# Attention with adaLN: the 24 conditioning products of the attention stage, tied to softmax steps one by one

## The chip, the cores and the metric

One core of one Trainium2 chip runs the kernel. The metric is device time in microseconds (us) of one execution; the times shown are medians of several executions. Matmuls run on TensorE (PE; PEld is its weight load), elementwise work on VectorE (DVE), ScalarE (ACT) and GpSimd (POOL). DMA transfers are issued from the queues of SyncE (SP) and GpSimd.

## The reference, cut to what matters

A decoder trunk of two layers, 512 tokens of width 1024: attention and a feed-forward block, then a gated DeltaNet and a feed-forward block. Every sub-layer is preceded by an RMSNorm whose scale and shift, and followed by a gate, that come from the condition vector c (adaLN):

```python
cond = jax.nn.silu(c)
for layer in range(DEPTH):
    mod = (cond @ ada_w[layer] + ada_b[layer])[:, None, :]
    shift_m, scale_m, gate_m, shift_f, scale_f, gate_f = jnp.split(mod, 6, axis=-1)
    h = rmsnorm(x, norm_mix_g[layer]) * (1.0 + scale_m) + shift_m
    mixed = attention_head_groups(h, ...) if layer % 2 == 0 else gated_deltanet(h, ...)
    x = x + gate_m * mixed
    h = rmsnorm(x, norm_ffn_g[layer]) * (1.0 + scale_f) + shift_f
    x = x + gate_f * swiglu(h, ffn_w_in[layer], ffn_w_out[layer])
```

The attention has eight softmax heads (MoBA) and eight stick-breaking heads of width 64 over the same 512 tokens, causal.

## The kernel before, in words

Everything is f32; a matmul is made of three, on operands split into a high and a low part (`split`, line 246, writes the high part on ACT and the low part on DVE).

The matrix-vector product of adaLN is not done on TensorE. `ada` (line 206) loads a block of 128x1024 weights (tile `aw`, 512 KB, issued from SP), and one DVE instruction multiplies it by `cond` and adds up along the row (line 214), with a second short one that writes the sum to a column of `mod`. There are 96 such blocks: 6 components times 8 chunks for each layer. The first 16 (shift and scale of the first norm) run at the start, 24 run in the attention stage (components 2, 3 and 4 of the first layer: the gate of the attention, shift and scale of the first feed-forward block), and 56 run in the first feed-forward block. In the attention stage `aw` has two buffers, so the load for one product can be issued only when the product two before it has run, and SP, which takes its queue in order, waits there.

The attention stage goes over four pairs p of heads, and over two heads h in each (called head 1 to head 8 here). A head is a softmax head, `moba` (line 749), followed by a stick-breaking head, `stick` (line 774). `moba` has four steps, one per block of 128 queries. A step is a chain across the engines: scores on PE (tile `s`, one buffer), the row maximum on DVE (line 759), the exponential with its row sum on ACT (line 761), the reciprocal on DVE (line 762), the scaling of the row by it on DVE (line 763, tile `p`), transposes on PE (line 767, tile `pt`, one buffer) and their split into `ph` and `pl`. Four steps done, `pv_out` multiplies by the values. `stick` is such a chain too, with tiles `z`, `u`, `ssh`, `ssl`, `sph`, `spl`.

While the chains of a pair run, PE has other matmuls in between: the projections of the next pair (`proj`, line 707; `spread` in line 702 ties each group of three matmuls to a matmul of a step), and in heads 7 and 8 a part of the output projection (lines 840 to 842). The weights of the projections come on GpSimd's queue, each in two transfers (lines 286 and 288, `wh` and `wl`); those of the output projection (`attn_out`, tile `raw`, line 292) come on SP's queue behind the `aw` loads.

Which instruction follows which on an engine is settled when the program is built, by a scheduler that simulates the engines and takes ready instructions by their place in the source. `tc.issue_after(x)` makes what stands in its block come after instruction x on x's engine. On the chip each engine runs its list strictly in order, and waits for semaphores.

Before the change `moba` returns the reciprocal of its last step, and the loop over heads places products after it, as many as the table says (lines 72 and 814 to 817):

```python
ADA = (0, 6, 6, 6, 6, 0, 0, 0)
```

so that six products are placed after the last softmax step of each of heads 2 to 5. `between` (line 830) would place what the table leaves over; the table leaves none.

Of the kernel before, what the change touches and what calls it, by code (L numbers as in the profile page):

```python
# [12 lines left out]
AF = mybir.ActivationFunctionType  # L13
OP = mybir.AluOpType
# [53 lines left out]
OG, NG = (6, 8), 18  # L68
GS = 4
ROT = 2  # L70
AENG = "v"
ADA = (0, 6, 6, 6, 6, 0, 0, 0)
NSPLIT = 4
NFIRST = 2
NFIRST_GDN = 2
# [55 lines left out]
def build(nc, tc, I, O):  # L131
    V, G, A, PE = nc.vector, nc.gpsimd, nc.scalar, nc.tensor
    from contextlib import ExitStack
    ctx = ExitStack()
    with ctx:
# [38 lines left out]
        apool = actx.enter_context(tc.tile_pool(name="apool", bufs=1))  # L174
        cond = apool.tile([128, D], F32, name="cond")
# [27 lines left out]

        mod = const.tile([128, 96], F32, name="mod")

        def ada(layer, comp, chunk, pool=apool, bufs=2, eng="v"):
            j = layer * 48 + comp * 8 + chunk
            w = pool.tile([128, D], F32, name="aw", tag="aw", bufs=bufs)
            nc.sync.dma_start(w, I["ada_w"][j])
            if eng == "g":  # L210
                ins = G.tensor_tensor(w, w, cond, op=OP.mult)
                A.activation(w, w, AF.Copy, accum_out=mod[:, j:j + 1])
                return ins
            return V.tensor_tensor_reduce(w, w, cond, 1.0, 0.0, OP.mult, OP.add, mod[:, j:j + 1])  # L214

        fin = const.tile([128, 96], F32, name="fin")
# [240 lines left out]
        env.__dict__.update(locals())  # L457

        xctx = attention(env, xctx)
        with ExitStack() as fctx:  # L460
            after = norm(1, 0, 1, hs)
# [73 lines left out]
def attention(e, x0ctx):  # L535
    nc, tc, V, G, A, PE, I = e.nc, e.tc, e.V, e.G, e.A, e.PE, e.I
    from contextlib import ExitStack
    with ExitStack() as ctx:
# [73 lines left out]
        with e.psum_pool("start") as sp:  # L612
            pq = [sp.tile([128, T], F32, name=f"pq{i}") if i < 1 else e.mm_tile() for i in range(4)]
            pv = [sp.tile([128, T], F32, name=f"pv{i}") for i in range(4)]
            with e.pool("rtmp") as tmp:
                for k in range(KC):
# [7 lines left out]
                    ins = e.norm_h(FULL, 0, 0, 1, hs, (k,))  # L624
# [3 lines left out]
                    a, z = k == 0, k == KC - 1  # L628
# [73 lines left out]
        def spread(n, u0, u1):  # L702

            s = [x for u in range(u0, u1) for x in steps[u]]
            e.gates[:] = [s[i * len(s) // n] for i in range(n)]

        def proj(pair, i):
            w = e.load_w(("attn_in", (pair - 1) * 4 + i))
            ps = e.mm_tile()
            e.gemm(ps, w, hs, FULL)  # L710
            return finish(ps, *KINDS[i])

        def vproj(i):
            ws = [e.load_w(("attn_v", i, j)) for j in (0, 4)]
            for c in range(4):
                ps = e.mm_tile()[:, :256]
                t = slice(c * 128, c * 128 + 128)
                for k in range(KC):
                    xh, xl = hs[k]
                    wh, wl = (w[:, k % 4] for w in ws[k // 4])  # L720
                    with e.behind() if k % 2 == 0 else ExitStack():
                        PE.matmul(ps, xh[:, t], wh, start=k == 0, stop=False)
                        PE.matmul(ps, xh[:, t], wl, start=False, stop=False)
                        PE.matmul(ps, xl[:, t], wh, start=False, stop=k == KC - 1)
                for j in range(2):
                    e.split(ps[:, j * 128:j * 128 + 128], *(t[:, c] for t in vtile("b", 2 * i + j)))

        def pv_out(chunk, r0, tag, ph, pl, at):

            o = psum.tile([128, T], F32, name="o", tag="o", bufs=1)  # L730
            vh, vl = vtile("ab"[chunk // 4], chunk % 4)
            for j in range(4):
                q = slice(j * 128, T)
                PE.matmul(o[:, q], vh[:, j], at(ph, j), start=j == 0, stop=False)
                PE.matmul(o[:, q], vl[:, j], at(ph, j), start=False, stop=False)
                PE.matmul(o[:, q], vh[:, j], at(pl, j), start=False, stop=j == 3)
            rs = slice(r0, r0 + 64)
            e.split(o[rs], ot[chunk][0][rs], ot[chunk][1][rs])

        def qk3(ps, k, ks, q, qs, at, mask):  # L740

            kh, kl = k
            qh, ql = q
            PE.matmul(ps, kh[:, ks], qh[:, qs], start=True, stop=False)
            PE.matmul(ps, kh[:, ks], ql[:, qs], start=False, stop=False)
            PE.matmul(ps[:, at], e.identb, mask, start=False, stop=False)
            steps[-1].append(PE.matmul(ps, kl[:, ks], qh[:, qs], start=False, stop=True).ins)

        def moba(pair, h, q, k):

            ph = work.tile([128, 1920], F32R, name="ph", tag="ph", bufs=1)
            pl = work.tile([128, 1920], F32R, name="pl", tag="pl", bufs=1)
            for i in range(4):
                n = 128 * (i + 1)
                qs = slice(i * 128, n)
                s = psum.tile([128, T], F32, name="s", tag="s", bufs=1)
                qk3(s[:, :n], q[h], qs, k, slice(0, n), qs, causal)
                st = work.tile([128, 3], F32, name="st", tag="st", bufs=4)
                V.tensor_reduce(st[:, 0:1], s[:, :n], AX.X, OP.max, negate=True)
                p = work.tile([128, T], F32, name="p", tag="p", bufs=2)  # L760
                A.activation(p[:, :n], s[:, :n], AF.Exp, bias=st[:, 0:1], accum_out=st[:, 1:2])
                ins = V.reciprocal(st[:, 2:3], st[:, 1:2])
                V.tensor_scalar(p[:, :n], p[:, :n], st[:, 2:3], None, op0=OP.mult)
                pt = psum.tile([128, T], F32, name="pt", tag="pt", bufs=1)
                for j in range(i + 1):
                    js = slice(j * 128, j * 128 + 128)
                    PE.transpose(pt[:, js], p[:, js], e.ident)
                src = pt[:, :n].rearrange("p (j q) -> p j q", q=128)
                e.split(src, *(x[:, i * 128:i * 128 + 384 * (i + 1)].rearrange("p (j q) -> p j q", q=384)[:, :, :128]
                               for x in (ph, pl)))  # L770
            pv_out(pair, h * 64, "m", ph, pl, lambda x, j: x[:, 512 * j:512 * j + 512 - 128 * j])
            return ins

        def stick(pair, h, q, k):
            off = {3: 0, 2: 128, 1: 384, 0: 768}
# [34 lines left out]
        for p in range(4):  # L810
            qa, ka, qb, kb = cur
            for h in range(2):
                steps.append([])
                ins = moba(p, h, qa, ka)
                for j in range(sum(ADA[:2 * p + h]), sum(ADA[:2 * p + h + 1])):
                    with tc.issue_after(ins.ins):
                        e.ada(0, 2 + j // 8, j % 8, eng=AENG[j % len(AENG)])
                stick(p, h, qb, kb)
            if p == 0:
                vproj(1)  # L820
            if p < 3:
                spread(32, 2 * p, 2 * p + 2)
                cur = [proj(p + 1, i) for i in range(4)]
# [4 lines left out]
        e.open_keep()  # L828

        def between(n, ins):  # L830
            a = sum(ADA)
            m = (24 - a) // 4
            for j in range(a + n * m, a + n * m + m):
                with tc.issue_after(ins.ins):
                    e.ada(0, 2 + j // 8, j % 8)
            if n == 3:
                e.ada_fin(0, 3)
                e.ada_fin(0, 4, gain=e.gffn[:, 0:8])

        s = [x for u in steps[OG[0]:OG[1]] for x in u]  # L840
        for i in range(3):
            e.gates += [s[(6 * i + j) * len(s) // NG] for j in range(6)] + 2 * [None]
        e.out_proj(lambda n: [e.load_w(("attn_out", n, 0))], ot, 0, 2, NSPLIT, e.norm(0, 3, 4, hs),
                   ORDER, between, keep=True)
    return xctx

# [471 lines left out]
```

## Time and profile before

| | |
|---|---|
| median of 3 runs | 1441.11 us (1438.31 to 1442.24) |
| profiled execution: its own time | 1445.06 us |
| profiled execution: span | 1443.2 us (1.86 us of its time lie outside the span) |
| PE busy | 1390.6 us (96%) |
| DVE busy | 831.2 us (58%) |
| ACT busy | 580.3 us (40%) |
| POOL busy | 337.4 us (23%) |

The busy shares are means over the whole span; the attention stage reaches from about 87 to 297 us. Where PE is not busy there, or runs at its lower clock, time is lost that nothing later can win back, as PE has work for nearly all of the rest.

### The profile page before, as it was taken

To read this page: it belongs to the slowest core of one execution; us is meant where nothing else is said; L and a number is where in the kernel's file an instruction comes from. 1 tells how busy PE (TensorE), PEld (TensorE's weight loads), DVE (VectorE), ACT (ScalarE), POOL (GpSimd) and SP (SyncE) were. 2 spreads that over 40 slices of the span, in tenths; PEclk is the share of its full clock that TensorE was granted. 3 is DMA by queue.
4 is the path that set the end of the run, shared out by engine and by line. 5 is a ranking of instruction groups with operands and counts; after the bars stand their busy time and mean duration, and the time that the engine had idled before them with its cause. 6 is when DMAs were issued, how large, how long until landed. Compare 5 with 4: busy or idle time off the path is not lost.

```text
span 1443.2 us, 19371 instructions
## 1 busy us (share of the span) xinstructions
PE 1390.6 (96%) x7418; PEld 1172.9 (81%) x7418; DVE 831.2 (58%) x1410; ACT 580.3 (40%) x1114; POOL 337.4 (23%) x336
## 2 busy tenths in 40 slices
PE   7999898999999999999899989999999999999997
PEld 4787677889888888888878877888998888888887
DVE  6776778646566566423777897436783333333233
ACT  4465565745222222222446743336662222222222
POOL 5023342213111111010424734311031111110010
PEclk8999999999999999999999999999999999999999
DMA  9437664042476666444522314312361332333332
GB/s 369 150 77 181 181 178 129 30 146 89 147 234 225 231 227 216 150 127 124 182 73 74 88 61 130 102 60 88 115 207 45 102 101 90 102 94 92 92 103 74
DMA packets 58734, 190.66 MB, mean 132 GB/s; under 512 B 7081, under 2 KB 11305, under 8 KB 58642
## 3 DMA queue, kind: packets, MB, share of 16 engines
q1 hardware_dynamic: 53376, 173.56, 37.1%
q0 software_dynamic: 4112, 14.82, 4.6%
q8 instruction: 58, 0.95, 0.3%
q10 hardware_dynamic: 1154, 1.05, 0.2%
q14 instruction: 34, 0.28, 0.1%
HBM read 184.11 MB, written 5.29 MB: 131 GB/s over the span
## 4 chain that ended last, share of the span: by engine, by line
PE 80%; DVE 8%; DMA 6%; ACT 3%; POOL 2%; issue 1%; SPq 0%; DVEq 0%; ACTq 0%; POOLq 0%
PE mm L332 20%; PE mm L333 20%; PE mm L335 20%; DMA aw<-in_ada_w_dram 3%; DVE aw L214 1%; PE mm L1126 1%; PE mm L1124 1%; PE mm L1125 1%; PE f L335 1%; PE bank L958 1%; DVE DT L1018 1%; DVE wl L254 1%; PE f L333 1%; PE f L332 1%; DMA call<-in_consts_dram 1%
## 5 line engine op out<-in xcount | busy, mean ns | idle before, releaser
L249 ACT ACTIVATE wh<-raw 128x1024 fp32r<-128x1024 f32 (+1 forms) x199 | 206.9, 1040 | 536.2 <-PE mm L333 493.1
L254 DVE TENSOR_TENSOR wl<-raw,wh 128x1024 fp32r<-128x1024 f32 (+1 forms) x193 | 234.1, 1214 | 195.7 <-ACT wh L249 175.4
L332 PE MATMUL mm<-hh,wh 128*128 128x512 f32 (+1 forms) x776 | 292.4, 381 | 0.2
L333 PE MATMUL mm<-hl,wh 128*128 128x512 f32 (+1 forms) x776 | 291.5, 379 | 0.0
L335 PE MATMUL mm<-hh,wl 128*128 128x512 f32 (+1 forms) x776 | 246.3, 378 | 0.4 <-DVE wl L254 0.4
L333 PEld LDWEIGHTS mm<-hl,wh 128*128 128x128 f32 x776 | 147.0, 190 | 27.6
L332 PEld LDWEIGHTS mm<-hh,wh 128*128 128x128 f32 x776 | 146.9, 190 | 26.9 <-ACT wh L249 0.3
L335 PEld LDWEIGHTS mm<-hh,wl 128*128 128x128 f32 x776 | 142.6, 189 | 29.4 <-DVE wl L254 0.6
L214 DVE CUSTOM_DVE_ANT_0 aw<-aw,cond 128x1024 f32<-128x1024 f32 x96 | 124.1, 1314 | 18.6 <-DMA aw<-in_ada_w_dram 18.5
L251 POOL TENSOR_SCALAR ah<-ac 128x512 fp32r<-128x512 f32 x36 | 53.3, 1481 | 330.4 <-DVE ac L496 330.4
L333 PE MATMUL mm<-al,wh 128*128 128x512 f32 (+1 forms) x354 | 124.6, 356 | 0.0
L332 PE MATMUL mm<-h1h,wh 128*128 128x512 f32 x320 | 124.5, 389 | 0.0
L333 PE MATMUL mm<-h1l,wh 128*128 128x512 f32 x320 | 124.5, 389 | 0.0
L332 PE MATMUL mm<-ah,wh 128*128 128x512 f32 (+1 forms) x354 | 124.2, 356 | 0.1
L496 DVE TENSOR_TENSOR ac<-sg,mm 128x512 f32<-128x512 f32 x40 | 27.5, 687 | 151.5 <-PE mm L335 151.5
L335 PE MATMUL mm<-h1h,wl 128*128 128x512 f32 x320 | 105.0, 389 | 0.0
L335 PE MATMUL mm<-ah,wl 128*128 128x512 f32 (+1 forms) x354 | 104.2, 356 | 0.0
L332 PEld LDWEIGHTS mm<-ah,wh 128*128 128x128 f32 x354 | 66.7, 189 | 9.7 <-ACT ah L249 0.4
L333 PEld LDWEIGHTS mm<-al,wh 128*128 128x128 f32 x354 | 66.8, 189 | 9.6
L335 PEld LDWEIGHTS mm<-ah,wl 128*128 128x128 f32 x354 | 64.2, 189 | 9.6 <-DVE wl L254 0.2
L335 PEld LDWEIGHTS mm<-h1h,wl 128*128 128x128 f32 x320 | 60.1, 188 | 12.5
L333 PEld LDWEIGHTS mm<-h1l,wh 128*128 128x128 f32 x320 | 60.1, 188 | 12.4
(403 smaller groups left out, 2557.7 us busy)
## 6 DMA issues: line engine op xcount, KB each, us to landing
aw<-in_ada_w_dram SPq DMA_DIRECT2D x96, 512.0 KB
raw<-in_ffn_in_dram SPq DMA_DIRECT2D x88, 512.0 KB
raw<-in_ffn_out_dram SPq DMA_DIRECT2D x36, 512.0 KB
raw<-in_gdn_in_dram SPq DMA_DIRECT2D x26, 512.0 KB
raw<-in_gdn_z_dram SPq DMA_DIRECT2D x16, 512.0 KB
raw<-in_gdn_out_dram SPq DMA_DIRECT2D x16, 512.0 KB
raw<-in_ffn_out_dram SPq DMA_DIRECT2D x18, 384.0 KB
wh<-in_attn_in_dram POOLq DMA_DIRECT2D x12, 512.0 KB, 4.1
```

The lines of the kernel that those rows point to most:

```text
L214: return V.tensor_tensor_reduce(w, w, cond, 1.0, 0.0, OP.mult, OP.add, mod[:, j:j + 1])
L249: ins = A.activation(h, src, AF.Copy)
L251: G.tensor_scalar(h, src, 1.0, 1.0, op0=OP.mult, op1=OP.mult)
L254: (G if eng == "p" else V).tensor_tensor(l, src, h.bitcast(F32), op=OP.subtract)
L332: PE.matmul(ps, wh[k][:, 0], xh[:, cs], start=first and i == 0, stop=False)
L333: PE.matmul(ps, wh[k][:, 0], xl[:, cs], start=False, stop=False)
L335: PE.matmul(ps, wl[j][:, 0], x[j][0][:, cs], start=False, stop=last and j == order[-1])
L496: ins = V.tensor_tensor(ac, sg, pu, op=OP.mult)
L958: PE.matmul(ps[:, c], lhs[:, cs], rhs[:, cs], start=True, stop=True)
L1018: V.tensor_tensor(d, DS[:, :m, m:m + 1].to_broadcast([128, m, w]), DV[:, m:m + 1, m:].to_broadcast([128, m, w]), op=OP.mult)
L1124: PE.matmul(p, xh[:, t], wh[:, k - j], start=k == 0, stop=False)
L1125: PE.matmul(p, xl[:, t], wh[:, k - j], start=False, stop=False)
```

## The change

The table and the loop that placed six products after a head's last reciprocal are taken out. Instead each of the four softmax steps of heads 2 to 7 places one product, after its own reciprocal and, in the source, ahead of the scaling. The products, their number (24) and their order are the same. The unused way of doing a product on GpSimd and the empty loop in `between` are removed too.

```diff
-ADA = (0, 6, 6, 6, 6, 0, 0, 0)
+ADA0 = 4
...
                 ins = V.reciprocal(st[:, 2:3], st[:, 1:2])
+                step = 4 * (2 * pair + h) + i - ADA0
+                if 0 <= step < 24:
+                    with tc.issue_after(ins.ins):
+                        e.ada(0, 2 + step // 8, step % 8)
                 V.tensor_scalar(p[:, :n], p[:, :n], st[:, 2:3], None, op0=OP.mult)
...
-                ins = moba(p, h, qa, ka)
-                for j in range(sum(ADA[:2 * p + h]), sum(ADA[:2 * p + h + 1])):
-                    with tc.issue_after(ins.ins):
-                        e.ada(0, 2 + j // 8, j % 8, eng=AENG[j % len(AENG)])
+                moba(p, h, qa, ka)
                 stick(p, h, qb, kb)
...
         def between(n, ins):
-            a = sum(ADA)
-            m = (24 - a) // 4
-            for j in range(a + n * m, a + n * m + m):
-                with tc.issue_after(ins.ins):
-                    e.ada(0, 2 + j // 8, j % 8)
```

Line numbers of the changed program are a little lower: its product is line 209 (before 214), its split's DVE half 249 (254), its reciprocal 757 (762), its scaling 762 (763), the `u` of `stick` 791 (793).

DVE's list before, from the first to the second softmax step of head 4 (`ISA` on `aw` is a product, the `ISA` on `mod` behind it writes its sum; `rq` is a projected q or k under rotation):

```order
L763 TENSOR_SCALAR p<-p,st 128x128
L214 ISA aw,mod<-aw,cond 128x1024
L214 ISA mod 128x1
L668 TENSOR_TENSOR rq<-rq,C 128x512
L254 TENSOR_TENSOR ssl<-u,ssh 128x512
L762 RECIPROCAL st<-st 128x1
L793 SCALAR_TENSOR_TENSOR u<-z,u 128x128
```

The same place of DVE's list in the changed program:

```order
L249 TENSOR_TENSOR ssl<-u,ssh 128x512
L663 TENSOR_TENSOR rq<-rq,C 128x512
L757 RECIPROCAL st<-st 128x1
L209 ISA aw,mod<-aw,cond 128x1024
L209 ISA mod 128x1
L664 TENSOR_TENSOR rq<-rq,rs 128x512
L762 TENSOR_SCALAR p<-p,st 128x256
```

The fifth product of the six placed after head 3 stood ahead of `ssl`, which head 3's stick-breaking part needs, and of the reciprocal; now the second product of head 4 stands between the reciprocal and the scaling, and `ssl` ahead of both. So it is in all 24 steps of heads 2 to 7: one product lies between reciprocal and scaling. Before, 12 of the 24 products lay between a reciprocal and its scaling, in heads 2 to 6, and none in head 7.

DVE's list at the first two steps of head 7, changed program:

```order
L757 RECIPROCAL st<-st 128x1
L209 ISA aw,mod<-aw,cond 128x1024
L209 ISA mod 128x1
L791 SCALAR_TENSOR_TENSOR u<-z,u 128x256
L762 TENSOR_SCALAR p<-p,st 128x128
L249 TENSOR_TENSOR ssl<-u,ssh 128x256
L791 SCALAR_TENSOR_TENSOR u<-z,u 128x384
L249 TENSOR_TENSOR bl_191<-o,bh_190 64x512
L754 TENSOR_REDUCE st<-s 128x1
```

Before, the scaling followed the reciprocal at once here, and no product stood in the head.

SP's queue before, from the loads of the value weights to those of x (a row with x18 is 18 loads in a row):

```order
L292 DMA raw<-in_attn_v_dram 128x1024 x4
L209 DMA aw<-in_ada_w_dram 128x1024 x18
L292 DMA raw<-in_attn_out_dram 128x1024
L209 DMA aw<-in_ada_w_dram 128x1024 x6
L292 DMA raw<-in_attn_out_dram 128x1024 x4
```

The same in the changed program:

```order
L287 DMA raw<-in_attn_v_dram 128x1024 x4
L208 DMA aw<-in_ada_w_dram 128x1024 x16
L287 DMA raw<-in_attn_out_dram 128x1024
L208 DMA aw<-in_ada_w_dram 128x1024
L287 DMA raw<-in_attn_out_dram 128x1024
L208 DMA aw<-in_ada_w_dram 128x1024 x2
L287 DMA raw<-in_attn_out_dram 128x1024
L208 DMA aw<-in_ada_w_dram 128x1024 x3
L287 DMA raw<-in_attn_out_dram 128x1024 x2
L208 DMA aw<-in_ada_w_dram 128x1024 x2
```

The five loads of output-projection weights now stand between the last eight `aw` loads instead of mostly behind them. The last two `aw` loads in either list are for the feed-forward block.

## Rows read from the trace of the kernel before

**Rows 1.** The page: span, and busy time of each engine.
```profile
span 1443.2 us, 19371 instructions
PE 1390.6 (96%) x7418; PEld 1172.9 (81%) x7418; DVE 831.2 (58%) x1410; ACT 580.3 (40%) x1114; POOL 337.4 (23%) x336
```
**Rows 2.** Busy time by stretch: heads 2 to 8, one line each.
```profile
core 0: us, PE busy (x) PEld busy (x) DVE busy (x) ACT busy (x) POOL busy (x), PEclk, DMA share, GB/s
103.70:138.10 34.40, 34.31 (x180) 28.34 (x179) 23.63 (x48) 21.55 (x48) 14.56 (x19) 1.00 0.67 158
138.10:163.90 25.80, 22.98 (x127) 18.41 (x127) 17.37 (x38) 14.44 (x35) 9.02 (x13) 1.00 0.69 197
163.90:192.30 28.40, 24.50 (x125) 20.10 (x124) 22.23 (x45) 15.38 (x37) 11.09 (x12) 0.88 0.62 169
192.30:220.00 27.70, 25.40 (x132) 20.50 (x131) 21.90 (x45) 15.89 (x37) 12.58 (x12) 0.94 0.78 203
220.00:244.40 24.40, 20.49 (x101) 15.93 (x100) 22.89 (x45) 14.47 (x34) 6.97 (x7) 0.95 0.48 160
244.40:264.10 19.70, 19.70 (x116) 16.47 (x114) 11.61 (x27) 13.50 (x34) 3.44 (x6) 0.97 0.17 54
264.10:297.20 33.10, 30.53 (x181) 25.32 (x181) 19.86 (x43) 24.37 (x63) 7.30 (x10) 1.00 0.00 1
```
**Rows 3.** Busy time by stretch: from the end of the attention to the end.
```profile
345.00:1443.00 1098.00, 1074.37 (x5675) 911.69 (x5673) 588.33 (x945) 379.57 (x672) 230.41 (x191) 0.99 0.39 124
```
**Rows 4.** Tile aw, 90 to 345 us: the products and their duration (min/median/max).
```profile
L214 DVE CUSTOM_DVE_ANT_0 aw<-aw,cond x24: 1195/1216/1764, 125.4 to 229.6; 128x1024 f32<-128x1024 f32 x24
```
**Rows 5.** Waits of DVE, 90 to 345 us: us in total, times, longest us.
```profile
DVE aw L214 <- DMA aw<-in_ada_w_dram: 13.2, 7, 4.1
```
**Rows 6.** Timeline at 174 us: start us, us, engine, instruction, [idle before <-releaser].
```profile
175.28 1.22 DVE L214 CUSTOM_DVE_ANT_0 aw<-aw,cond 128x1024 f32<-128x1024 f32 x1 [2.90 <-DMA aw<-in_ada_w_dram]
177.03 0.68 DVE L254 TENSOR_TENSOR ssl<-u,ssh 128x512 fp32r<-128x512 f32 x1
177.77 0.79 PE L799 MATMUL z<-ssl,ntri 128*128 128x512 f32 x1 [3.18 <-DVE ssl L254]
```
**Rows 7.** Timeline, three more waits of PE behind a late DVE, and what held DVE.
```profile
144.35 0.38 PE L744 MATMUL s<-kah,qah 128*128 128x256 f32 x1 [2.01 <-ACT p L761]
...
205.45 1.23 DVE L214 CUSTOM_DVE_ANT_0 aw<-aw,cond 128x1024 f32<-128x1024 f32 x1 [1.45 <-DMA aw<-in_ada_w_dram]
...
207.81 0.73 PE L799 MATMUL z<-ssl,ntri 128*128 128x512 f32 x1 [1.99 <-DVE ssl L254]
...
241.72 0.33 PE L744 MATMUL s<-kah,qah 128*128 128x128 f32 x1 [2.32 <-ACT p L761]
```
**Rows 8.** Busy time by stretch of 4 us: granted clock around waits of PE.
```profile
140.00:144.00 4.00, 2.33 (x16) 1.89 (x14) 1.64 (x4) 0.16 (x1) 0.26 (x1) 1.00 1.03 293
176.00:180.00 4.00, 1.51 (x3) 1.00 (x4) 4.00 (x10) 1.99 (x6) 0.00 (x0) 0.65 0.46 146
180.00:184.00 4.00, 4.00 (x11) 2.80 (x11) 3.94 (x10) 1.26 (x2) 2.21 (x3) 0.50 0.43 135
208.00:212.00 4.00, 4.00 (x12) 2.87 (x13) 3.38 (x8) 1.59 (x6) 1.89 (x2) 0.58 0.91 222
240.00:244.00 4.00, 2.28 (x7) 1.91 (x8) 4.00 (x8) 2.26 (x6) 1.68 (x2) 0.76 0.40 123
244.00:248.00 4.00, 4.00 (x21) 3.35 (x20) 1.51 (x4) 2.12 (x8) 0.22 (x1) 0.82 0.02 8
```
**Rows 9.** Chain that ended last: two transfers of aw, start us, us.
```profile
135.14 10.49 DMA aw<-in_ada_w_dram
...
225.56 4.06 DMA aw<-in_ada_w_dram
```
**Rows 10.** Timeline of DVE in head 7: reciprocals of its first and third step.
```profile
248.09 0.15 DVE L762 RECIPROCAL st<-st 128x1 f32<-128x1 f32 x1
...
257.90 0.15 DVE L762 RECIPROCAL st<-st 128x1 f32<-128x1 f32 x1
```

More of the change, by code (lines that the diff above doesn't have):

```diff
@@ L70 @@
 ROT = 2
-AENG = "v"
-ADA = (0, 6, 6, 6, 6, 0, 0, 0)
+ADA0 = 4
 NSPLIT = 4
@@ L204, in build, with ada @@
         mod = const.tile([128, 96], F32, name="mod")
-        def ada(layer, comp, chunk, pool=apool, bufs=2, eng="v"):
+        def ada(layer, comp, chunk, pool=apool, bufs=2):
             j = layer * 48 + comp * 8 + chunk
@@ L209, in ada @@
             nc.sync.dma_start(w, I["ada_w"][j])
[L210 to L213, printed above, removed]
             return V.tensor_tensor_reduce(w, w, cond, 1.0, 0.0, OP.mult, OP.add, mod[:, j:j + 1])
@@ L771, in moba @@
             pv_out(pair, h * 64, "m", ph, pl, lambda x, j: x[:, 512 * j:512 * j + 512 - 128 * j])
-            return ins
         def stick(pair, h, q, k):
```

## The prediction, made before the changed kernel ran

> **What bounds the kernel now.** I read the page first. PE is busy for 96% of the span, DVE for 58% [rows 1]. The reader should see that no other engine can set the end for the kernel as a whole, so a change of DVE's order can be worth only what PE loses somewhere. After the attention, PE is idle for 1098.00 - 1074.37 = 23.6 us of 1098 at a granted clock of 0.99 [rows 3], and the change touches nothing there. So that part only moves earlier or later as a whole.
>
> The stretches by head come next [rows 2]. In heads 2 and 7 PE is never idle (0.09 us and 0). In heads 3 to 6 it is idle for 25.80 - 22.98 = 2.82, 28.40 - 24.50 = 3.90, 27.70 - 25.40 = 2.30 and 24.40 - 20.49 = 3.91 us, together 12.9 us, and the granted clock drops to 0.88 in head 4. The products placed after heads 2 to 5 run there.
>
> Third, what ends those waits. DVE waits 13.2 us in 7 cases for the load of a product [rows 5]. At 174 us it stands before a product for 2.90 us, runs it for 1.22 us, then does another instruction and the `ssl` of head 3, and only then can PE's next matmul run: PE had waited 3.18 us [rows 6]. At 205.45 it is the same, with 1.99 us of PE waiting [rows 7]. The waits of 2.01 and 2.32 us behind an exponential [rows 7] come from a late row maximum on DVE: at 144 us because of a product that waited for its load, at 241 us because DVE is behind with its list after the last six products (22.89 of 24.40 us busy in head 6 [rows 2]).
>
> Fourth, the clock. After the waits at 174 to 179 us the stretch 180 to 184 us runs at a granted clock of 0.50, that is all at 1.2 GHz, the lower of the two levels; 208 to 212 us has 0.58, 240 to 248 us 0.76 and 0.82 [rows 8]. The work lost in a stretch is half of the time that PE works at the lower level: 4 x 0.50 = 2.0, 4 x 0.42 = 1.7, 4 x 0.24 = 1.0, 4 x 0.18 = 0.7, and for 176 to 180 us, where PE was busy for 1.51 us only, at most 0.75. Together 6.1 us. The 2.01 us wait at 142 us left the clock at 1.00 [rows 8], so a short wait need not cost this.
>
> **The change part by part.** (a) Six products in a burst on two buffers are taken apart. The third to sixth of a burst had to wait for a load that could be issued only when the product two before had run; two such transfers took 10.49 and 4.06 us [rows 9]. With one product per step, the same load has two steps. In head 7, which no product disturbs, reciprocals one and three are 257.90 - 248.09 = 9.8 us apart [rows 10]; less the product, 8.5 us are left for a transfer. That covers the 4.06 us end and falls short of the 10.49 us end by 2.0 us. I take it that most loads arrive in time, and that the waits of PE in heads 3 to 6 go, with the clock they cost: -12.9 - 6.1 = -19.0 us. This is the upper bound of this term as well; its lower bound is 0, should every wait return at another place.
>
> On the load's time the Trainium skill (DMA: Bandwidth & Descriptors, section Bandwidth) states 6.15 us for 1 MB at 341 GB/s, which is two of these loads at once. By that figure, as an estimate, no product would wait at all, and the sum would be 2 us lower than mine, -15.0 us. The trace's 10.49 us for one load speaks for some waits that remain.
>
> (b) What is given back in heads 3 to 6. A product costs DVE 1.22 us [rows 4] and 0.08 us for its sum, so 1.30 us. Now all 24 lie between a reciprocal and its scaling, where 12 did: 12 x 1.30 = 15.6 us longer chains in all, which is the upper bound if PE has nothing else to do in any of them. The lower bound is nothing, from head 2: four products ran in its stretch, one of its scalings stood behind two of them, and PE was idle for 0.09 us [rows 2]. I take 1 us per head, nearer to head 2, because projections lie between the steps there, and half of it for loads that still come late: +4 us. DVE's total work does not change.
>
> (c) Head 7 gets four products that it did not have: 4 x 1.30 = 5.2 us on DVE, 11.61 + 5.2 = 16.8 of 19.70 us, or 85%. Heads 4 and 5 with 78 and 79% lost 3.9 and 2.3 us, partly to the loads. Bounds 0 (PE was never idle here) and 5.2 (nothing hides them); I take 2 us. Head 2's four products stand earlier than before, beside projections that hide them: 0.
>
> (d) The queues. On SP, five loads of output-projection weights now stand between the last eight `aw` loads, so they wait until products of heads 5 to 7 have run. Their first use is at the end of head 6 and in head 7, and the loads of x, which come behind, were issued only at the end of head 8. GpSimd's list hardly changes. 0 us. The removed code on GpSimd was never run: 0. The columns for the feed-forward norm are complete at the end of head 7 instead of in head 6, with all of head 8 (33.10 us [rows 2]) before anything reads them: 0.
>
> Sum: -19.0 + 4 + 2 = -13.0 us. The profiled execution took 1445.06 us, 4.0 us above the median of the runs; against its own time the result is 1432.1, against the median of 1441.11 us it is **1428 us**.
>
> **The rivals.** *The waits stay* (about 1438 us). The `aw` loads compete with GpSimd's transfers of projection weights; in heads 3 to 5 the DMA engines are busy for 62 to 78% [rows 2]. If most transfers then take as long as the 10.49 us one, each product waits about 2 us in its place between reciprocal and scaling, instead of in a burst. DVE waited 13.2 us in all before; 2 us at, say, 6 of the 24 products would nearly restore that, and of the 19.0 us only the backlog of head 6 and its clock would go: 3.9 + 1.7, less 2 in head 7, so about -3.5 us. For it: the load that took 10.49 us. Against it: before, two loads were usually in flight together because products ran back to back, now mostly one. The Trainium skill (DMA: Bandwidth & Descriptors, section Issuing engines are not separate DMA queues) says that transfers of all engines share the same 16 DMA engines and interleave, which is the rule behind this rival; no run here yet shows one load alone.
>
> *The softmax chain becomes the bound* (about 1450 us, slower). Each step of heads 2 to 7 is 1.30 us longer before its transposes can run. If PE runs out of other matmuls in each, the 15.6 us of (b) show in full, and a wait in each of six heads pulls the clock down as at 180 us, 2.0 us each: 15.6 + 12 - 19.0 = +8.6 us. It decides from the point where the waits of a head are long enough to lower the clock, so above the 2 us that left it at 1.00. For it: head 7 has the fewest other matmuls and gets four new products. Against it: heads 2 and 7 show no idle PE at all, and the row maximum and exponential of the next step do not need the scaling of this one.
>
> That the change does not do what it says is excluded: in the order of the changed program each of the 24 reciprocals of heads 2 to 7 is followed by one product.
>
> **How the numbers follow.** About 0.3%, 4.3 us, is what a measurement of this kernel can tell from no change. The forecast, with gains between 6 and 22 us (all of the 19.0, and the 2.6 us that PE idles in head 8 at most), has a chance of 0.72, all of it faster. *The waits stay* has 0.16, half of it just faster and half the same. *The chain* has 0.12, with 0.09 slower and 0.03 the same, where only part of it shows. So faster 0.80, same 0.11, slower 0.09. The range goes from 1419 (22 us gained) to 1439 us, which takes in the first rival and leaves out the second.
>
> **What would show it.** Right: DVE's wait for `aw` well under 13.2 us; PE idle for about 1 us in each of heads 3 to 6 and 2 us in head 7; no stretch at a granted clock near 0.50 in the attention; head 4 shorter than 28.40 us by 4 us or more; the time after the attention unchanged. Wrong: waits of PE for transposes behind a scaling that stands behind a product (the chain), or DVE waiting for loads in many steps (the first rival), or as many microseconds lost again in heads 7 and 8.

## The result, and the profile after

The changed kernel takes 1430.39 us (median of 4 runs, 1428.88 to 1430.72), the kernel before 1439.9 us (median of 4, 1438.31 to 1442.24): a ratio of 0.992 with an interval of 0.9902 to 0.9938. Run again, it took 1429.95 us against 1441.98, 0.9923 (0.9898 to 0.9948). The change makes the kernel 0.8% faster. The prediction was 1428 us in a range of 1419 to 1439. (Further down, one execution of the bursts without loads took 4601.09 us and one with pairs 4674.71; why is open, and leaving them out moves the medians by less than 0.2 us.)

The page of the changed kernel's profiled execution (1430.58 us):

```profile
span 1428.8 us, 19361 instructions
PE 1386.5 (97%) x7418; PEld 1171.3 (82%) x7418; DVE 830.1 (58%) x1410; ACT 581.2 (41%) x1114; POOL 336.8 (24%) x336
```

DVE does the same work as before [rows 1], in a shorter span. Busy time by stretch, heads 2 to 8, columns as in [rows 2]:

```profile
103.10:137.50 34.40, 34.40 (x181) 28.57 (x180) 23.26 (x48) 22.00 (x48) 16.06 (x19) 1.00 0.70 173
137.50:162.10 24.60, 22.79 (x127) 18.74 (x127) 16.94 (x39) 13.68 (x34) 8.18 (x12) 1.00 0.68 187
162.10:185.50 23.40, 22.61 (x129) 18.67 (x128) 20.69 (x42) 16.40 (x40) 9.22 (x12) 1.00 0.69 181
185.50:206.50 21.00, 21.00 (x122) 17.59 (x121) 17.16 (x38) 15.26 (x37) 8.93 (x12) 1.00 0.64 160
206.50:228.90 22.40, 21.35 (x119) 17.54 (x118) 22.04 (x42) 15.25 (x36) 9.03 (x9) 1.00 0.52 160
228.90:249.80 20.90, 20.90 (x127) 17.96 (x126) 18.75 (x42) 15.77 (x40) 8.03 (x9) 1.00 0.53 175
249.80:281.90 32.10, 29.19 (x159) 23.09 (x157) 18.48 (x42) 21.59 (x55) 5.69 (x8) 0.95 0.05 17
```

Heads 3 to 6 took 106.3 us before [rows 2] and take 91.4 us now. PE is idle there for 1.81 + 0.79 + 0 + 1.05 = 3.65 us instead of 12.9, and the granted clock is 1.00 in all four. Head 7, which got four products, is 1.2 us longer, with PE never idle. The time before head 3 is 0.6 us shorter, head 8 is 1.0 us shorter, and what comes behind it takes 1146.9 us instead of 1146.0. The longest waits of DVE (90 to 345 us; us in total, times, longest) and the rows of the products:

```profile
DVE x L405 <- PE mm L330: 10.0, 7, 2.8
DVE u L791 <- ACT u L790: 8.3, 8, 2.2
```
```profile
L209 DVE CUSTOM_DVE_ANT_0 aw<-aw,cond x24: 1195/1206/2323, 105.6 to 247.7; 128x1024 f32<-128x1024 f32 x24
```

The two rows are the longest waits; a row like [rows 5] is not in the list at all: DVE waits for none of the 24 loads. What is new is at the end of head 8, where the stick-breaking chain ends and PE has little else (busy time in stretches of 4 us):

```profile
276.00:280.00 4.00, 2.57 (x7) 1.48 (x7) 0.98 (x2) 1.23 (x2) 0.00 (x0) 0.84 0.00 0
280.00:284.00 4.00, 3.32 (x13) 2.80 (x12) 1.10 (x2) 1.65 (x2) 0.00 (x0) 0.50 0.18 67
284.00:288.00 4.00, 4.00 (x16) 3.22 (x15) 2.99 (x4) 2.64 (x3) 0.00 (x0) 0.81 1.03 338
```

The granted clock drops here, which it did not in the same place before (head 8 at 1.00 [rows 2]). By the prediction's way of counting that is about 4 x 0.16 + 4 x 0.50 + 4 x 0.19 = 3.4 us, less what PE was idle anyway. PE's longest wait there is only 1.35 us. So one of the prediction's signs of being right, no stretch near 0.50 in the attention, did not come.

### The profile page after: what moved, and what is told of

Same layout as the page of the kernel before. It is cut to its first block, busy times and chain, and to the rows that moved or that the text cites. A ratio compares the mean times of both kernels' runs of the same rounds, so it can differ in the third digit from the quotient of the medians.

```text
span 1428.8 us, 19361 instructions
## 1 busy us (share of the span) xinstructions
PE 1386.5 (97%) x7418; PEld 1171.3 (82%) x7418; DVE 830.1 (58%) x1410; ACT 581.2 (41%) x1114; POOL 336.8 (24%) x336
## 3 DMA queue, kind: packets, MB, share of 16 engines
q10 hardware_dynamic: 1154, 1.05, 0.2%
## 4 chain that ended last, share of the span: by engine, by line
PE 83%; DVE 8%; ACT 3%; DMA 3%; POOL 1%; issue 1%; SPq 0%; DVEq 0%; ACTq 0%; POOLq 0%
PE mm L327 21%; PE mm L328 21%; PE mm L330 20%; PE z L797 1%; PE mm L1116 1%; PE mm L1114 1%; PE mm L1115 1%; PE bank L948 1%; PE f L330 1%; DVE DT L1008 1%; DVE wl L249 1%; PE f L328 1%; PE f L327 1%; DMA wh<-in_attn_in_dram 1%; DMA call<-in_consts_dram 1%
## 5 line engine op out<-in xcount | busy, mean ns | idle before, releaser
L348 POOL TENSOR_TENSOR ssq<-ssq,sq 128x512 f32<-128x512 f32 x14 | 21.1, 1508 | 212.1 <-ACT sq L344 212.1
```

The source lines that it names most:

```text
L348: eng.tensor_tensor(ssq[:, cs], ssq[:, cs], sq[:, cs], op=OP.add)
```

## The experiments

Two theories stood after the result. *Loads*: the kernel before lost its time because DVE waited 13.2 us for the loads of products that came in bursts on two buffers. *Burst*: it lost it because a row of products on DVE delays what stands behind the row, wherever the loads are.

A yardstick for all of them is how far PE gets in one fixed stretch, 137.5 to 250 us: the number of its instructions there, the first (x...) in a row. It is read from the profiled execution, which is not always near the median (with pairs it took 1438.49 us, 4 us more than the median), and it does not count what is won or lost outside the stretch. The kernel before:

```profile
137.50:250.00 112.50, 99.57 (x518) 80.38 (x517) 87.05 (x177) 63.81 (x152) 40.41 (x45) 0.94 0.62 175
```

The changed kernel:

```profile
137.50:250.00 112.50, 108.84 (x617) 90.62 (x617) 95.77 (x199) 76.56 (x184) 43.39 (x50) 1.00 0.62 173
```

**Bursts without loads.** The burst of the kernel before, with 22 of the 24 loads left out.

```diff
+        held = {}
...
+            w = held.get(j % 2) if hold else None
+            if w is not None:
+                return V.tensor_tensor_reduce(w, cond, cond, 1e-3, 0.0, OP.mult, OP.add, mod[:, j:j + 1])
...
-                        e.ada(0, 2 + j // 8, j % 8, eng=AENG[j % len(AENG)])
+                        e.ada(0, 2 + j // 8, j % 8, hold=True)
```

> The kernel before, with its bursts of six products, but 22 of the 24 loads in the attention stage are left out: those products multiply cond by itself (scaled by 0.001), so these columns are not the reference's. Same DVE instructions at the same places, nothing to wait for. If the loss of the kernel before came from DVE waiting for loads (loads theory): PE idle in heads 3 to 6 falls from 12.9 us to under 5, time 1429 to 1434 us. If it came from six products standing in a row on DVE, whatever the loads (burst theory): the time stays within 1436 to 1440 us.

Measured: 1448.33 us against 1441.72, ratio 1.0048 (1.0032 to 1.0064). It is slower than the kernel before, which neither theory had. The expectation was wrong in one point: the places were not the same. With no load to wait for, the scheduler packed the six products more closely. The timeline of DVE shows six of them within 14.2 us, 158.77 to 172.97 us, around one row maximum:

```profile
158.77 1.21 DVE L212 CUSTOM_DVE_ANT_0 aw<-cond 128x1024 f32<-128x1024 f32 x1
...
159.90 1.22 DVE L212 CUSTOM_DVE_ANT_0 aw<-cond 128x1024 f32<-128x1024 f32 x1
...
162.69 1.33 DVE L212 CUSTOM_DVE_ANT_0 aw<-cond 128x1024 f32<-128x1024 f32 x1
...
163.96 4.59 DVE L212 CUSTOM_DVE_ANT_0 aw<-cond 128x1024 f32<-128x1024 f32 x1
...
169.61 0.28 DVE L767 TENSOR_REDUCE st<-s 128x1 f32<-128x128 f32 x1
...
170.41 1.21 DVE L212 CUSTOM_DVE_ANT_0 aw<-cond 128x1024 f32<-128x1024 f32 x1
...
171.76 1.21 DVE L212 CUSTOM_DVE_ANT_0 aw<-cond 128x1024 f32<-128x1024 f32 x1
```

And the timeline of PE, with its idle time and what ended it in brackets:

```profile
170.43 0.53 PE L752 MATMUL s<-kah,qah 128*128 128x256 f32 x1 [2.34 <-ACT p L769]
```

The row maximum of head 4's first step stands behind the fourth product, and PE waits 2.34 us for the exponential behind it. No wait for a load is needed for that. But the fourth product took 4.59 us instead of 1.21 (see the last section), which is more than PE waited, so this place does not show what a row costs by itself. Head 5's first step does so better: four products begin between 186.31 and 192.25 us, the longest takes 1.88 us, the row maximum stands behind the fourth, and PE waits 1.69 us.

```profile
192.25 1.21 DVE L212 CUSTOM_DVE_ANT_0 aw<-cond 128x1024 f32<-128x1024 f32 x1
...
193.40 0.28 DVE L767 TENSOR_REDUCE st<-s 128x1 f32<-128x128 f32 x1
...
194.47 0.58 PE L752 MATMUL s<-kah,qah 128*128 128x256 f32 x1 [1.69 <-ACT p L769]
```

So a close row of products can cost without any wait for a load; whether the waits of the kernel before cost something too, this run can't say.

**Bursts of four.** The table of the kernel before set to four products after each of heads 2 to 7.

```diff
-ADA = (0, 6, 6, 6, 6, 0, 0, 0)
+ADA = (0, 4, 4, 4, 4, 4, 4, 0)
```

> The kernel before with the table (0, 4, 4, 4, 4, 4, 4, 0): four products in a row after the last step of heads 2 to 7, loads as they are. Loads theory: the third and fourth of each burst still wait for loads that were issued only after the first and second, so DVE waits 6 to 10 us for loads and the time is 1434 to 1438 us. Burst theory (less work in a row, spread over six heads): 1430 to 1433 us, like the changed kernel.

Measured: 1437.26 us against 1441.72, ratio 0.9968 (0.9949 to 0.9987). The time is the one that the loads theory gave, its reason is not: DVE waits for loads 2.1 us in all, not 6 to 10.

```profile
DVE aw L214 <- DMA aw<-in_ada_w_dram: 2.1, 3, 1.1
```

With the waits nearly gone and the same heads as in the changed kernel, 7 us remain between this and 1430 us. (Its ten runs are spread wide, 1431.98 to 1444.79 us.)

**Behind the scaling.** The changed kernel with the product taken off the softmax chain.

```diff
-                ins = V.reciprocal(st[:, 2:3], st[:, 1:2])
+                V.reciprocal(st[:, 2:3], st[:, 1:2])
+                ins = V.tensor_scalar(p[:, :n], p[:, :n], st[:, 2:3], None, op0=OP.mult)
                 step = 4 * (2 * pair + h) + i - ADA0
...
-                V.tensor_scalar(p[:, :n], p[:, :n], st[:, 2:3], None, op0=OP.mult)
```

> The changed kernel with each product tied to the scaling of its step instead of to the reciprocal, so that it stands behind the scaling, off the softmax chain. If the 1.30 us between reciprocal and scaling cost PE time (chain rival), this is 3 to 6 us faster than the changed kernel: 1424 to 1427 us. If other matmuls hide them: the same within 2 us, 1429 to 1432 us.

Measured: 1433.58 us against 1441.72, ratio 0.9945 (0.993 to 0.996). It is no faster than the changed kernel, so the 1.30 us between reciprocal and scaling cost PE nothing that could be had back in this way. The time lies above both forecasts, 1424 to 1427 and 1429 to 1432 us. DVE waits for no load here either, and the products stand one by one, so neither theory gives the 3 to 4 us above the changed kernel; their cause is open. An edit of this kind also lets the scheduler order the other instructions anew, (217 of DVE's 326 rows of the changed kernel keep their order), and nothing in this run keeps the two apart.

**One buffer.** The spread kept, the waits put back.

```diff
-        def ada(layer, comp, chunk, pool=apool, bufs=2):
+        def ada(layer, comp, chunk, pool=apool, bufs=1):
...
-                    e.ada(*x)
+                    e.ada(*x, pool, 2)
```

> The changed kernel with one buffer for aw in the attention stage instead of two (the products of the feed-forward block keep two, in that block's own memory). Each load can be issued only when the product one step before has run; about 4.5 us remain for a load of 4 to 10 us. Loads theory: DVE waits 1 to 3 us before most of the 24 products, over 20 us in all, and the time is 1438 to 1455 us, back at the kernel before or above. Burst theory: the spread is kept, 1429 to 1434 us.

Measured: 1442.1 us against 1441.72, ratio 1.0008 (0.9992 to 1.0023): the whole gain is gone. DVE waits for loads 10.4 us in 13 cases, half of what I expected, and PE gets to x562 in the stretch of the yardstick:

```profile
DVE aw L209 <- DMA aw<-in_ada_w_dram: 10.4, 13, 2.3
```
```profile
137.50:250.00 112.50, 103.85 (x562) 83.81 (x560) 86.03 (x177) 69.15 (x165) 39.94 (x46) 1.00 0.60 160
```

So waits for loads seem to cost when they happen, even with the products one by one (heads 1 to 6, below, gives a better comparison). Neither theory alone holds for both this run and the first.

**The changed kernel again, and pairs.** The second is the changed kernel with two products on every second step.

```diff
-                if 0 <= step < 24:
-                    with tc.issue_after(ins.ins):
-                        e.ada(0, 2 + step // 8, step % 8)
+                if 0 <= step < 24 and step % 2:
+                    for j in (step - 1, step):
+                        with tc.issue_after(ins.ins):
+                            e.ada(0, 2 + j // 8, j % 8)
```

> The changed kernel itself, once more, beside the others of this call: 1429 to 1433 us, 0.990 to 0.994 of the kernel before.

> The changed kernel with two products behind the second and the fourth reciprocal of each of heads 2 to 7 instead of one behind each of the four. Burst theory (what a row of products on DVE delays is what costs, so it grows with the length of the row: one 1430, four 1437, six 1440 us): between, 1431 to 1435 us. Loads theory (the rows cost nothing where the loads are there, and with bursts of four DVE did not wait for one): 1429 to 1432 us, no different from one by one.

Measured against 1441.98 us: 1429.95 us, 0.9923 (0.9898 to 0.9948), and 1434.44 us, 0.9949 (0.9934 to 0.9963). Pairs lie where the burst theory put them, and DVE waits for no load there. But they are only 1 us above the single products behind the scaling (1433.58 us), so this does not yet tell a row of two from a new order of the rest. The stretch of pairs, for the yardstick:

```profile
137.50:250.00 112.50, 108.37 (x588) 88.90 (x586) 91.62 (x183) 71.98 (x169) 44.64 (x49) 0.97 0.60 165
```

**Single products without loads, and no products.** The first is the control of the first experiment, with the same edit in the changed kernel; the second leaves the 24 products out.

```diff
+        G.memset(mod[:, 16:40], 0.0)
...
-                if 0 <= step < 24:
+                if 0 <= step < 0:
```

> The changed kernel with 22 of the 24 loads of the attention stage left out in the same way as in the bursts without loads (cond by itself, scaled by 0.001; those columns are not the reference's). It is the control of that run. Burst theory: leaving out the loads does not matter where DVE does not wait for them, so 1428 to 1433 us; the bursts without loads were slow (1448 us) because of the bursts. If this run too is slower than the changed kernel by 5 us or more, it is the way in which the loads were left out that costs, and the run of bursts without loads tells nothing.

> The changed kernel without the 24 products and loads of the attention stage (their columns are set to 0, so gate, shift and scale there are not the reference's). It bounds what products cost when they stand one by one. Burst theory: PE has other matmuls for most of the 1.30 us, so this is only 2 to 6 us faster than the changed kernel, 1424 to 1428 us. If 24 single products still cost much, 10 us or more: under 1420 us.

Measured against 1441.98 us: 1428.73 us, 0.9915 (0.9892 to 0.9938), and 1427.96 us, 0.9906 (0.9881 to 0.9931). Leaving out the loads in this way does no harm, so the first experiment was slow because of where its products stand: in close rows, some of them stretched. What its 24 products take beyond 1.21 us each adds up to 6.4 us, against 2.2 us here, so the stretching is hardly the whole of the 19.6 us between the two runs. And 24 products with their loads, one by one, cost 2 us in all (1429.95 - 1427.96), at the low end of the expectation; the runs of the two programs overlap. The stretch without products:

```profile
137.50:250.00 112.50, 110.03 (x627) 92.15 (x625) 78.49 (x159) 77.76 (x187) 38.40 (x50) 1.00 0.36 85
```

DVE is busy for 17 us less than in the changed kernel, and PE gets only 10 instructions further. PE is idle for 112.50 - 110.03 = 2.47 us here, without any product, and for 3.66 us in the changed kernel.

**The old list without loads.** Nearer to what the first experiment should have been: each product tied to its place among the softmax and stick-breaking steps in DVE's list of the kernel before, and 22 loads left out.

```diff
+        at_m = {12: 2, 20: 1}
+        at_r = {7: 2, 8: 1, 11: 2, 15: 2, 17: 1, 19: 2, 20: 1, 21: 1}
+        at_s = {12: 1, 13: 1, 16: 1, 20: 1}
+        at_u = {6: 2, 7: 1, 14: 1, 15: 1}
...
+                put(at_r.get(step, 0), ins)
```

(Step number: count of products behind its row maximum, reciprocal, scaling, and stick-breaking step.)

> The 24 products tied to the places that they have in DVE's list of the kernel before (two or one behind a reciprocal, a row maximum, a scaling or a stick-breaking step, so the list is the same within a few rows), and 22 of the 24 loads left out as before (cond by itself, those columns are not the reference's). Only the waits for loads are gone. Loads theory (my prediction's term: 12.9 us of idle PE and 6.1 us of clock came from them): 1428 to 1433 us. Burst theory (the rows of products cost by themselves): 1437 to 1442 us. Between, both count, and the distance to the kernel before is what the waits cost.

Measured: 1432.99 us (1432.01 to 1435.79) against 1441.06, ratio 0.9947 (0.9927 to 0.9968). It is in the loads theory's band, at its upper end.

```profile
137.50:250.00 112.50, 105.08 (x565) 85.90 (x565) 92.91 (x187) 71.78 (x166) 46.22 (x47) 0.97 0.37 89
```

The time is 1441.06 - 1432.99 = 8.1 us under the kernel before, and 4.3 us above the single products without loads (1428.73 us). Read as the loads theory and the burst theory have it, 8.1 us are the waits for loads and 4.3 us the rows of products. The lists do not allow that much. The products stand where they stood, 12 of them between a reciprocal and its scaling as before, but it is not true that the list is the same within a few rows. In the traces from 84 to 300 us, 231 of DVE's 318 rows of before stand in the same order in both (the longest sequence that the two have in common), and 795 of PE's 1034; two executions of the changed kernel agree in 325 of 326 and 1089 of 1105. And the three programs with single products, their loads and no wait for them (the changed kernel, behind the scaling, and heads 1 to 6 below) lie between 1429.95 and 1433.58 us. So 8.1 us is more than these differ among themselves, and some of it is most likely the waits; how much is not shown, and the 4.3 us are not shown to be the rows. (PE's x565 is close to the x562 of one buffer, which took 1442.1 us: here the yardstick misses what is won outside its stretch.)

**Heads 1 to 6.** An attempt at a faster version.

```diff
-ADA0 = 4
+ADA0 = 0
```

> The changed kernel with the 24 products one step earlier by a head (heads 1 to 6 instead of 2 to 7). Head 7, which has the fewest other matmuls, is free of products again, and head 1 gets four. If head 7's four products cost 1 to 2 us, as the prediction took: 1428 to 1430 us. If singles cost nothing anywhere: 1429 to 1432 us, the same as the changed kernel. If the first loads come late behind those of the start: 1432 to 1436 us.

Measured: 1432.99 us (1431.64 to 1439.57) against 1441.06, ratio 0.994 (0.9919 to 0.9962). It is not faster than the changed kernel. DVE does not wait for loads here, so the cause that I named for this time isn't it; the cause is open. The run serves for something else. Its order is close to that of one buffer (269 of 317 rows of DVE and 936 of PE's 1072 in the same order, though its products begin a head earlier), and it has none of that run's 10.4 us of waits for loads: 1432.99 us against 1442.1. That is the closest comparison here for what such waits cost, single products in both. With 1427.96 us as the time without any product, there is little left to gain by moving them.

## Why the prediction was right

*Time and sign.* 13.0 us were forecast. The profiled executions differ by 1445.06 - 1430.58 = 14.5 us, the medians by 9.5 and, run again, by 12.0 us. The profiled execution of before was one of its longer ones: 20 runs of it beside the first experiments lay between 1436.23 and 1446.40 us, the 8 runs of the changed kernel between 1428.88 and 1430.72. The sum was made against that execution, and its idle time and slow clock were at the high end. Why the runs of the kernel before spread so much more was not tried.

*What was luck.* For heads 3 to 6 the sum had -19.0 + 4 = -15.0 us, and they are 14.9 us shorter. The parts do not fit as well as their sum. Without any product the kernel gains 1441.98 - 1427.96 = 14.0 us, so (a) with its 19.0 us was too large; and all 24 single products cost 2.0 us, not the 4 + 2 = 6 us of (b) and (c). The two errors, 5 and 4 us, nearly cancel.

*(a) The waits go, with their clock: 19.0 us.* The direction holds: of the 12.9 us of idle PE in heads 3 to 6, 3.65 are left, the clock there is 1.00 throughout, and DVE waits for no load. It could not all go: 2.47 us of idle PE stay even without products. The reason was half of it. That waits for loads cost is shown in kind (one buffer against heads 1 to 6, and the old list without loads, 8.1 us with its order changed). That rows of products cost without such waits, which (a) knew only as a means to make loads late and as the backlog of head 6, is shown by the bursts without loads, which are slower than the kernel before (1448 us). How the gain divides between the two is not shown. Single products (1430 us), pairs (1434) and fours (1437) rise as rows would have it, but single products in another order reach 1433.6 us too.

*(b) 4 us given back in heads 3 to 6.* PE is idle there for 3.65 us, which looks like the size, but 2.47 us of idle time are there without products as well, so little of it is given back by them. Half of the term was for late loads, and none came late. The Trainium skill (DMA: Bandwidth & Descriptors, Bandwidth) gives 6.15 us for a transfer of 1 MB issued from GpSimd, and by the estimate made from it no product was to wait; the trace agrees, as no load is waited for, but no run here shows the time of two loads alone. The 10.49 us transfer [rows 9] was one of a pair: the products behind the two loads began at 142.37 and 145.65 us, and GpSimd issued projection weights at 133.47 and 138.63 us.

*(c) 2 us in head 7.* The head is 1.2 us longer, but no time was lost in it: PE is busy for all of its 20.90 us at a clock of 1.00 (0.97 before) and runs 127 instructions instead of 116. The expected 2 us of idle PE are not there.

*(d) Queues: 0.* Nothing waits for the output-projection weights that had to pass between the loads before head 8 has ended.

*Not foreseen:* the lower clock at the end of head 8, some 3 us in the profiled execution. "As many microseconds lost again in heads 7 and 8" was named as a way to be wrong, with no price. The head is 1.0 us shorter all the same, and the run without products has a lower clock there too (0.71 and 0.87 from 276 to 284 us), so the products are not needed for it.

*The rivals.* The waits stay: no, though one buffer brings waits back and loses the whole gain. The chain: no, since leaving the products out altogether gains only 2 us; taking them off the chain (behind the scaling) gains nothing. The point from which the chain was to decide, waits above 2 us, does not follow from the rows: the wait of 1.99 us at 206 us [rows 7] was followed by a granted clock of 0.58 [rows 8].

## What to carry to other kernels

Side work on an engine that is busy for 58% on average can be all but free if it is placed one piece at a time, each behind a fixed instruction of the main chain (24 products of 1.2 us cost 2 us here, 5 to 6 us in two other arrangements of single products), and dear in close rows (up to 18 us here, stretched products among them). Each piece should be placed so that its buffer's next load has more time than the transfer takes: with one buffer less, which brought the waits back, the whole gain was lost. An experiment that takes a wait away in a scheduled program also lets the scheduler order the rest anew, even where the pieces themselves are tied down. So the lists of all engines are to be compared before the times are, and a difference of 3 or 4 us is not put down to one cause while the order differs.

## What was not expected of the hardware

A product of 1.21 us took 4.59 us in the bursts without loads. GpSimd ran four instructions one after another during that time (timeline at 164 us, the same run):

```profile
164.34 1.58 POOL L675 TENSOR_TENSOR rs<-rs,S 128x512 f32<-128x512 f32 x1
...
165.58 1.30 POOL L814 TENSOR_TENSOR spl<-sq,sph 128x384 fp32r<-128x384 f32 x1
...
166.55 0.92 POOL L813 TENSOR_SCALAR sph<-sq 128x512 fp32r<-128x512 f32 x1
...
167.55 2.12 POOL L814 TENSOR_TENSOR spl<-sq,sph 128x512 fp32r<-128x512 f32 x1
```

The product ended at 168.55 us, during the fourth. The next DVE instruction, of 8 columns, took 1.21 us and ended with the fourth. In the changed kernel the slowest product took 2.32 us and the median was 1.206. Over all traces (264 products in the attention stage), the 150 with no GpSimd work (issues of transfers apart) at the same time took 1.19 to 1.23 us; of the 67 that overlap one of its TENSOR_TENSOR instructions, 45 took more than 1.3 us. The Trainium skill (GPSIMD Engine Reference, Specifications) says that GpSimd's interfaces to SBUF are shared with VectorE, and that instructions with two SBUF inputs contend with it; a product is one of those. The rows and the count fit that, but no run here moved GpSimd's work away, so the cause is not shown.
